# Retention values and gate projected by one 512-column job at the head of the kernel

## The chip, the core and the metric

One Trainium2 chip, one core of it. The metric is the time of one execution of the whole program on the device, in microseconds (us). Five engines run side by side, each with its own queue of instructions, worked off in order: TensorE (PE in the profile, with its weight loads as PEld), VectorE (DVE), ScalarE (ACT), GpSimd (POOL) and SyncE (SP, which issues the DMAs). They wait for each other through semaphores.

## The reference, cut to what matters

A decoder layer: one projection of the input, three mixers side by side, an output projection, layer norm, an MLP and a second layer norm. All in float32, 1024 tokens of width 1024.

```python
z = x @ w_in                                        # 1024 x 1024 @ 1024 x 2816
u, rq, rk, rv, rg, aq, ak, av = jnp.split(z, ...)   # 256 columns each up to rg, then 512 each
y_ssm = rms_norm(s5_mixer(u, ...), ssm_norm)        # a complex diagonal scan over the tokens
y_ret = retention_mixer(rq, rk, rv, rg, ret_norm)   # chunks of 128 tokens; silu(rg) * norm(o)
y_att = rms_norm(dilated_attention_mixer(aq, ak, av), attn_norm)
h = concatenate([y_ssm, y_ret, y_att]) @ w_out
x = layer_norm(ALPHA * x + h)
x = layer_norm(ALPHA * x + square(relu(x @ w1)) @ w2)
```

`rv` (columns 768 to 1023 of `w_in`) are the values of the retention, `rg` (columns 1024 to 1279) is its gate. They lie side by side.

## The kernel before

A float32 product is made of three passes of TensorE: both operands are split into a rounded part and a rest (`hi` and `lo`), and `mm3` (L403) adds hi x hi, hi x lo and lo x hi in PSUM. The split of a weight tile is a cast on ACT (`whi`) and a subtraction (`wlo`) that `sub_lo` (L427) gives to DVE or POOL, whichever it thinks is free first. For the input the two parts are `XA` and `XB`, split tile by tile in `split_x` (L475) from the loaded `xt`.

The input projection is a list of jobs (`JOBS`, L53). A "chunk" job (`tm_groups`, L489) gives token-major results of 256 columns: eight token tiles of 128, each summed over eight pieces `k` of the contraction, with 24 matmuls of 256 columns, two tiles to a PSUM bank. A "tile" job (`fm_groups`, L504) gives 128 features by 512 tokens, with matmuls of 512 columns. The order is: rv (job 0), rk and rq for two halves, rg (job 5), u twice, av, then aq, ak and av for the attention. Job 0 is special: x tile 0 and the two weight chunks are loaded alternately in small pieces (`load_x` L463, `load_w` L516, `split_w` L538), so that TensorE can begin early. Results are taken out of PSUM by `ev_rv` (an ACT copy, L586) and `ev_rg` (ACT tanh into `rgth`, then a DVE `scalar_tensor_tensor` into `sg`, L592).

Beside these jobs run: `ssm_params` (L700), a long chain of small DVE instructions on `par` tiles, then products `V` and `CA`, with a few transposes on PE in between (`ps_prm`, `ps_vt`, `ps_c`) and small matmuls (`ps_k`) at its end; `ssm`, which begins with 32 matmuls into `ps_X` from the u jobs, then a scan on DVE and POOL (`X`, `park`, `Sx`, `wz`), ACT copies into `Ss` and matmuls into `ps_y`; `retention` in four steps of two chunks (PE `ps_z`, `ps_sT`, `ps_kv`, `ps_ro`, `ps_rT`; DVE `rkz`, `at`, `R`, `st`, `mv`, `on`; POOL `rst` and `on` times `sg`); the attention; and from about 400 us on the output projection (`MB` operands first, then `wah`/`wal`), then the MLP.

Nothing of this order is written out by hand. The parts are coroutines with a rank each, and a planner (`Stream`, L244) that runs when the program is built keeps an estimated clock for each engine and always emits the next instruction that could start earliest, ranks breaking ties. Ranks near 0 are the retention (0) and the S5 mixer (1); the projection jobs (10) fill the gaps on PE. The order so found is fixed in each engine's queue: on the chip an instruction that is not ready holds up all that stands behind it.

Of the kernel before, what the change touches and what calls it, by code (L numbers as in the profile page):

```python
# [13 lines left out]
F32R = mybir.dt.float32r  # L14
# [30 lines left out]
PICK = 2  # L45
NORMP = 0
ACTB = 0
JOBB = 15
VALA = 28
VALV = 4  # L50
WAG = "xb4.0"

JOBS = [("chunk", 768)] + [("tile", c + 128 * p) for p in range(2) for c in (512, 256)]  # L53
JOBS += [("chunk", 1024), ("tile", 0), ("tile", 128), ("chunk", 2304)]
JOBS += [("tile", c + 128 * p) for p in range(2) for c in (1280, 1792)] + [("chunk", 2560)]
JOBS += [("tile", c + 128 * p) for p in (2, 3) for c in (1280, 1792)]
LN2_HI = 0.693359375
# [240 lines left out]
async def when(w, early=0.0):  # L298
    if isinstance(w, str):
        await ask(("flag", w))  # L300
    elif w:
        await ask(("data", w, early))
# [3 lines left out]
def trunk_kernel(ctx: ExitStack, tc: tile.TileContext, t_in, out):  # L306
# [43 lines left out]
    def free(*tiles):  # L350

        for t in tiles:
            if isinstance(t, (list, tuple)):
                free(*t)
            else:
                room = st_.room[tags.pop(t.tensor.name)]
                room[0] += 1
                room[1].append(clock.last[t.tensor.name])
# [4 lines left out]
    async def Us(n, shape, dt=F32, name="u", spare=2):  # L363
        return [await U(shape, dt, name, spare) for _ in range(n)]
# [62 lines left out]
    async def sub_lo(lo, raw, hi, pick=PICK):  # L427

        await when([hi, raw])
        n = int(np.prod(lo.shape[1:]))  # L430
        t, r = clock.t, clock.ready([hi, raw], [lo])
        r = max(r, t.get("port", 0.0))
        late = max(t.get("dve", 0.0), r) + pick + 0.00104 * n > max(t.get("pool", 0.0), r) + 0.0021 * n
        await tt(pool if late else dve, lo, raw, f(hi), SUB)
# [28 lines left out]
    async def load_x():  # L463
        for t in range(8):
            xts[t] = await U([128, NKT, 128], name="xt")
            for a in range(XP[t]):
                n = NKT // XP[t]
                k = slice(n * a, n * a + n)
                await sp.dma_start(out=xts[t][:, k], in_=x_t[t][:, k])
                flag(f"xload{t}.{a}")  # L470
                if t == 0:
                    await when(f"wload0.{a}")
            flag(f"xload{t}")

    async def split_x():  # L475
# [13 lines left out]
    async def tm_groups(hl, done):  # L489
        for tp in range(4):  # L490
            ps = await PM((128, 2, 256))
            for i in range(2):
                t = 2 * tp + i
                tok = slice(t * 128, (t + 1) * 128)
                for k in range(NKT):
                    if k % (NKT // XP[t]) == 0:
                        await when(f"x{t}.{k}")
                    if t == 0 and k % 2 == 0:
                        await when(f"w0.{k}")
                    wh, wl = hl[k // 4]  # L500
                    await mm3(ps[:, i], XA[:, k, tok], XB[:, k, tok], wh[:, k % 4], wl[:, k % 4], k == 0, k == NKT - 1)
            done(tp, ps)

    async def fm_groups(hl, done):  # L504
        wh, wl = hl[0]
# [5 lines left out]
            done(th, ps)  # L511

    wraw, wsplit = {}, {}
    w_shape = {"chunk": [128, 4, 256], "tile": [128, NKT, 128]}

    async def load_w():  # L516
        u = 0
        for j, (kind, _) in enumerate(JOBS):
            if j > 1:
                await when(f"job{j - LOADW}")  # L520
            wraw[j] = []
            for i in range(2 if kind == "chunk" else 1):
                src = w_in[u].rearrange("p (a b) -> p a b", a=w_shape[kind][1])
                u += 1
                raw = await U(w_shape[kind], name="wraw", spare=4 if j > 1 else 0)
                wraw[j].append(raw)
                if j == 0:
                    for k in range(0, 4, 2):
                        await when(f"xload0.{2 * i + k // 2}")
                        await sp.dma_start(out=raw[:, k:k + 2], in_=src[:, k:k + 2])  # L530
                        flag(f"wload0.{2 * i + k // 2}")
                else:
                    await sp.dma_start(out=raw, in_=src)
            flag(f"wload{j}")
            if j == 0:
                await when("xload5")

    async def split_w():  # L538
        for j, (kind, _) in enumerate(JOBS):
            if j == 0:  # L540
                whl = await Us(4, w_shape[kind], F32R, "w0", spare=0)
                wsplit[0] = [whl[0:2], whl[2:4]]
                flag("wsplit0")
                for i in range(2):
                    await when(f"wload0.{2 * i}")
                    raw, (hi, lo) = wraw[0][i], whl[2 * i:2 * i + 2]
                    for k in range(0, 4, 2):
                        await when(f"wload0.{2 * i + k // 2}")
                        await act.copy(hi[:, k:k + 2], raw[:, k:k + 2])
                        await sub_lo(lo[:, k:k + 2], raw[:, k:k + 2], hi[:, k:k + 2], 0.0)  # L550
                        flag(f"w0.{4 * i + k}")
                    free(raw)
                continue
            await when(f"wload{j}")
            await when(f"job{j - 1}")
            wsplit[j] = [await w_split(w, w_shape[kind]) for w in wraw.pop(j)]
            flag(f"wsplit{j}")

    async def evacuate(j, groups, evac, name, queue):
        for i in range(2 if groups is fm_groups else 4):  # L560
            await when(f"sum{j}.{i}")
            await evac(i, queue[i])
        if name:
# [19 lines left out]

    T = {}

    async def ev_rv(tp, ps):  # L586
        if tp == 0:
            T["rv"] = await Us(2, [128, 4, 256], name="rv", spare=0)
        await act.copy(T["rv"][tp // 2][:, 2 * (tp % 2):2 * (tp % 2) + 2], ps)
        free(ps)  # L590

    async def ev_rg(tp, ps):  # L592
        if tp == 0:
            T["sg"] = await Us(2, [128, 4, 256], name="sg", spare=0)
        th = await H([128, 2, 256], name="rgth")
        await act.activation(th, ps, AF.Tanh, scale=0.5)
        await stt(T["sg"][tp // 2][:, 2 * (tp % 2):2 * (tp % 2) + 2], th, 1.0, ps, A_, M)
        free(th, ps)

    def ev_rq(p):  # L600
# [50 lines left out]
        return g  # L651


    jobs = [(tm_groups, ev_rv, "rv")]
    for p in range(2):
        jobs += [(fm_groups, ev_rk(p), None), (fm_groups, ev_rq(p), None if p == 0 else "rqk")]
    jobs += [(tm_groups, ev_rg, "rg"), (fm_groups, ev_u(0), None), (fm_groups, ev_u(1), "u"), (tm_groups, ev_av(0), "av0")]

    def qk_jobs(p):
        return [(fm_groups, ev_qk(p, "aq", -0.125), None), (fm_groups, ev_qk(p, "ak", 1.0), f"qk{p}")]  # L660
# [419 lines left out]
    async def retention():  # L1080
# [7 lines left out]
        for np_ in range(4):  # L1088
# [72 lines left out]
                        mv[:, i, h, 0:1], rst[:, i, h:h + 1], SUB, M)  # L1161
            free(po, mv, rst)
            if sg is None:
                await when("rg")
                sg = T["sg"]
            await tt(pool, on, on, sg[np_ // 2][:, 2 * (np_ % 2):2 * (np_ % 2) + 2], M)
            await when([on])
# [967 lines left out]
def host_arrays(inputs):  # L2135

    src = {n: np.ascontiguousarray(inputs[n]) for n in _INS}
    kp = lambda w: w.reshape(w.shape[0] // 128, 128, -1).transpose(1, 0, 2)
    src["x_t"] = np.ascontiguousarray(inputs["x"][0].reshape(8, 128, 8, 128).transpose(0, 3, 2, 1))
    w = inputs["w_in"][0]  # L2140
    units = []
    for kind, c0 in JOBS:
        if kind == "tile":
            units.append(kp(w[:, c0:c0 + 128]))
        else:
            units += [kp(w[a * 512:(a + 1) * 512, c0:c0 + 256]) for a in range(2)]
    src["w_in_units"] = np.stack([np.ascontiguousarray(u).reshape(128, 1024) for u in units])
    src["mlp_w1_units"] = np.ascontiguousarray(
        inputs["mlp_w1"][0].reshape(8, 128, 32, 128).transpose(2, 1, 0, 3).reshape(32, 128, 1024))
    src["mlp_w2_units"] = np.ascontiguousarray(  # L2150
        inputs["mlp_w2"][0].reshape(8, 2, 2, 128, 2, 512).transpose(2, 4, 0, 3, 1, 5).reshape(4, 8, 128, 1024))
    two = lambda n: inputs[n][0].reshape((8, 2) + inputs[n].shape[2:])
    col = lambda n: inputs[n][0].reshape(-1, 128).T
    pad = lambda v: np.concatenate([v, np.zeros((128 - v.shape[0], v.shape[1]), v.dtype)])
    src["params"] = np.concatenate(
        [two("ssm_b_" + n).transpose(1, 2, 0, 3).reshape(128, 128) for n in ("re", "im")]
        + [two("ssm_c_" + n).transpose(0, 2, 1, 3).reshape(128, 128) for n in ("re", "im")]
        + [pad(inputs["ssm_d"][0].reshape(8, 2, 16).transpose(1, 2, 0).reshape(32, 8))]
        + [col(n) for n in ("ret_out_norm", "ssm_out_norm", "ssm_b_glu", "ssm_b_glu", "attn_out_norm")], 1)
    src["rates"] = np.concatenate([two("ssm_lambda_re").reshape(8, 128), two("ssm_lambda_im").reshape(8, 128),  # L2160
                                   two("ssm_log_dt")], 1)
    src.update(shape_tables())
    return src
# [16 lines left out]
```

## Time and profile before

| | us |
|---|---|
| median of 3 runs | 1170.29 (1166.64 to 1170.9) |
| the profiled execution, its own time | 1170.03 |
| its span in the trace | 1168.3 |
| PE busy | 1122.4 (96%) |
| DVE busy | 814.3 (70%) |
| ACT busy | 532.3 (46%) |
| POOL busy | 239.4 (20%) |

The span is what the engines' records cover; 1.7 us of the execution lie around it. The rows of a trace are of this one execution. A matmul's duration in them overlaps with the next one's: the pace of PE is the distance from start to start. "Idle before, releaser" is the time for which the engine had nothing to do before an instruction, and what it had waited for.

### The profile page before, as it was taken

What the parts mean: (1) busy time and instruction counts of PE and PEld (TensorE: products, weight loads), DVE (VectorE), ACT (ScalarE), POOL (GpSimd) and SP (SyncE); (2) the same over time, 40 slices, a digit from 0 to 9 for tenths busy, and PEclk for the clock granted to TensorE, in tenths of its full rate; (3) what the DMA queues carried; (4) which work ended last, traced back from release to release, by engine and by line L of the source; (5) the groups of instructions that cost most, each with busy time, mean ns of one, the idle gap of its engine ahead of it and who ended that gap; (6) DMA issues with size and microseconds to landing.
All of it is one profiled execution on the core that took longest, in us unless ns stands there. A gap on an engine that the chain in (4) does not pass through costs nothing.

```text
span 1168.3 us, 15903 instructions
## 1 busy us (share of the span) xinstructions
PE 1122.4 (96%) x5825; PEld 950.5 (81%) x5825; DVE 814.3 (70%) x1665; ACT 532.3 (46%) x941; POOL 239.4 (20%) x183
## 2 busy tenths in 40 slices
PE   8999999899999989999999999999999999999996
PEld 7889888778888777887778888888788888888875
DVE  5986567676563688899776766667457785675865
ACT  5121322676756657336445454545444343442530
POOL 1232316635164533466000000000000000000104
PEclk9999999899999999999999999999999999999989
DMA  8000421520151624034263444434598667767521
GB/s 320 19 1 31 137 74 49 194 92 19 37 182 64 226 90 153 33 122 163 98 219 143 173 150 155 156 142 154 180 350 333 199 202 248 270 223 263 191 81 72
DMA packets 65133, 175.36 MB, mean 150 GB/s; under 512 B 7064, under 2 KB 16800, under 8 KB 65056
## 3 DMA queue, kind: packets, MB, share of 16 engines
q1 hardware_dynamic: 65056, 174.35, 42.6%
q8 instruction: 46, 0.75, 0.3%
q14 instruction: 31, 0.25, 0.1%
HBM read 127.42 MB, written 46.91 MB: 149 GB/s over the span
## 4 chain that ended last, share of the span: by engine, by line
PE 44%; DVE 4%; DMA 1%; issue 1%; ACT 1%; SPq 0%; DVEq 0%; POOL 0%
PE ps L394 27%; PE pm L394 17%; DVE dol L234 1%; DVE X L234 1%; DMA wraw<-in_mlp_w_units 1%; DMA rraw<-r_d 0%; DVE rs L234 0%; DMA K<-in_mlp_w_units 0%; DVE wop L234 0%; DVE SQ L234 0%; DVE ws L234 0%; ACT rb L234 0%; ACT X L234 0%; ACT doh L234 0%; DVE rb L234 0%
## 5 line engine op out<-in xcount | busy, mean ns | idle before, releaser
L234 POOL TENSOR_TENSOR lnr<-lnr,nhalf 128x1 f32<-128x1 f32 x16 | 10.9, 684 | 592.8 <-DVE lnmv L234 530.1
L394 PE MATMUL ps<-xoh,wop 128*128 128x512 f32 x384 | 123.7, 390 | 1.8 <-DVE u L234 1.8
L394 PE MATMUL pm<-doh 128*128 128x512 f32 x256 | 100.9, 394 | 3.0 <-DVE X L234 3.0
L234 ACT CAST doh<-rraw 128x1024 fp32r<-128x1024 f32 x56 | 58.7, 1049 | 93.2 <-DMA rraw<-r_d 73.2
L394 PE MATMUL pm<-dol,doh 128*128 128x512 f32 x256 | 100.8, 394 | 0.0
L394 PE MATMUL pm<-doh,dol 128*128 128x512 f32 x256 | 100.7, 393 | 0.0
L394 PE MATMUL pm<-XOB,wop 128*128 128x512 f32 x384 | 95.2, 393 | 0.2 <-DVE wop L234 0.2
L394 PE MATMUL ps<-XOA,wop 128*128 128x512 f32 x384 | 91.2, 390 | 3.6 <-DVE wop L234 3.6
L234 DVE TENSOR_TENSOR dol<-rraw,doh 128x1024 fp32r<-128x1024 f32 x56 | 68.4, 1221 | 33.0 <-ACT doh L234 33.0
L394 PE MATMUL pm<-XA,whi 128*128 128x512 f32 x224 | 89.3, 399 | 0.0
L394 PE MATMUL pm<-XA,wlo 128*128 128x512 f32 x224 | 88.6, 396 | 0.0
L394 PE MATMUL pm<-XB,whi 128*128 128x512 f32 x224 | 88.5, 395 | 0.0
L394 PEld LDWEIGHTS ps<-XOA,wop 128*128 128x128 f32 x384 | 71.9, 188 | 19.7 <-DVE wop L234 4.8
L394 PEld LDWEIGHTS ps<-xoh,wop 128*128 128x128 f32 x384 | 72.1, 188 | 17.4 <-DVE u L234 2.2
L234 ACT ACTIVATE rb<-rb 128x512 f32<-128x512 f32 x64 | 40.5, 633 | 98.6 <-DVE rb L234 97.6
L394 PEld LDWEIGHTS pm<-XOB,wop 128*128 128x128 f32 x384 | 71.0, 188 | 14.6 <-DVE wop L234 0.6
L234 POOL TENSOR_TENSOR wlo<-wraw,whi 128x1024 fp32r<-128x1024 f32 x24 | 58.3, 2440 | 104.2 <-ACT whi L234 83.9
L394 PE MATMUL ps<-xol,wop 128*128 128x512 f32 x192 | 74.7, 389 | 0.0
L394 PE MATMUL ps<-doh 128*128 128x512 f32 x192 | 74.7, 389 | 0.0
L394 PE MATMUL ps<-dol,doh 128*128 128x512 f32 x192 | 74.7, 389 | 0.0
L394 PE MATMUL ps<-doh,dol 128*128 128x512 f32 x192 | 74.7, 389 | 0.0
L394 PEld LDWEIGHTS pm<-doh 128*128 128x128 f32 x256 | 48.6, 190 | 14.3 <-issue 2.8
(286 smaller groups left out, 2802.9 us busy)
## 6 DMA issues: line engine op xcount, KB each, us to landing
wraw<-in_mlp_w_units SPq DMA_DIRECT2D x92, 512.0 KB
rraw<-r_d SPq DMA_DIRECT2D x56, 512.0 KB
r_d<-rs SPq DMA_DIRECT2D x32, 512.0 KB
wraw<-in_w_in_units SPq DMA_DIRECT2D x20, 512.0 KB
v_d<-v SPq DMA_DIRECT2D x8, 512.0 KB
w<-v_d SPq DMA_DIRECT2D x8, 512.0 KB
abias<-in_c_bias SPq DMA_DIRECT2D x8, 512.0 KB
wraw<-in_w_out SPq DMA_DIRECT2D x8, 512.0 KB
```

Source lines behind the costliest of these rows:

```text
L234: fn(*a, **kw)
L394: nc.tensor.matmul(ps, a, b, start=start, stop=stop, skip_group_check=open_)
```

## The change

rv and rg become one job, the first: eight token tiles, each with 24 matmuls of 512 columns into a whole PSUM bank (`wide_groups`), 192 in place of 2 x 192 of 256 columns. Its weights are four units of 256 rows by 512 columns, loaded in eight pieces (one for each `k`) instead of four pieces of two; x tile 0 is loaded as before, between them. `ev_rvg` takes the left half of each bank with an ACT copy and the right half with tanh on ACT and the multiply on DVE: eight of each on 256 columns, in place of four of each on 512. The job of rg after rq is gone, and so u follows rq directly. `JOBB` counts the same job as before.

```diff
-JOBB = 15
+JOBB = 14
-JOBS = [("chunk", 768)] + [("tile", c + 128 * p) for p in range(2) for c in (512, 256)]
-JOBS += [("chunk", 1024), ("tile", 0), ("tile", 128), ("chunk", 2304)]
+JOBS = [("wide", 768)] + [("tile", c + 128 * p) for p in range(2) for c in (512, 256)]
+JOBS += [("tile", 0), ("tile", 128), ("chunk", 2304)]
...
+    async def wide_groups(hl, done):
+        for t in range(8):
+            ps = await PM()
+            tok = slice(t * 128, (t + 1) * 128)
+            for k in range(NKT):
+                if k % (NKT // XP[t]) == 0:
+                    await when(f"x{t}.{k}")
+                if t == 0:
+                    await when(f"w0.{k}")
+                wh, wl = hl[k // 2]
+                await mm3(ps, XA[:, k, tok], XB[:, k, tok], wh[:, k % 2], wl[:, k % 2], k == 0, k == NKT - 1)
+            done(t, ps)
...
-                    for k in range(0, 4, 2):
-                        await when(f"xload0.{2 * i + k // 2}")
-                        await sp.dma_start(out=raw[:, k:k + 2], in_=src[:, k:k + 2])
-                        flag(f"wload0.{2 * i + k // 2}")
+                    await when(f"xload0.{i}")
+                    for k in range(2):
+                        await sp.dma_start(out=raw[:, k], in_=src[:, k])
+                        flag(f"wload0.{2 * i + k}")
...
-    async def ev_rv(tp, ps):
-        if tp == 0:
+    async def ev_rvg(t, ps):
+        if t == 0:
             T["rv"] = await Us(2, [128, 4, 256], name="rv", spare=0)
-        await act.copy(T["rv"][tp // 2][:, 2 * (tp % 2):2 * (tp % 2) + 2], ps)
-        free(ps)
-
-    async def ev_rg(tp, ps):
-        if tp == 0:
             T["sg"] = await Us(2, [128, 4, 256], name="sg", spare=0)
-        th = await H([128, 2, 256], name="rgth")
-        await act.activation(th, ps, AF.Tanh, scale=0.5)
-        await stt(T["sg"][tp // 2][:, 2 * (tp % 2):2 * (tp % 2) + 2], th, 1.0, ps, A_, M)
+        th = await H([128, 256], name="rgth")
+        await act.copy(T["rv"][t // 4][:, t % 4], ps[:, 0:256])
+        await act.activation(th, ps[:, 256:512], AF.Tanh, scale=0.5)
+        await stt(T["sg"][t // 4][:, t % 4], th, 1.0, ps[:, 256:512], A_, M)
         free(th, ps)
...
-    jobs = [(tm_groups, ev_rv, "rv")]
+    jobs = [(wide_groups, ev_rvg, "rv")]
...
-    jobs += [(tm_groups, ev_rg, "rg"), (fm_groups, ev_u(0), None), (fm_groups, ev_u(1), "u"), (tm_groups, ev_av(0), "av0")]
+    jobs += [(fm_groups, ev_u(0), None), (fm_groups, ev_u(1), "u"), (tm_groups, ev_av(0), "av0")]
```

Because the planner orders everything, the change moves instructions far beyond these lines. From the last part of the attention on (3004 PE instructions before the end, of 5421 now and 5613 before) PE's order is the same in both; ahead of that it is not. Three places.

VectorE at the start, between the split of x (`XB`) and the first instructions of the S5 parameters (`par`). Before:

```order
L234 TENSOR_TENSOR XB<-xt,XA 128x4x128 x2
L234 TENSOR_TENSOR XB<-xt,XA 128x8x128 x6
L234 COPY cols<-small 128x12
L234 COPY par<-small 8x256
L234 TENSOR_SCALAR cols<-cols 128x2 x3
L234 COPY par<-small 8x128
L234 COPY par<-ps_prm 128x24
```

and now:

```order
L234 TENSOR_TENSOR XB<-xt,XA 128x4x128 x2
L234 SCALAR_TENSOR_TENSOR sg<-rgth,pm 128x256
L234 TENSOR_TENSOR XB<-xt,XA 128x8x128 x4
L234 SCALAR_TENSOR_TENSOR sg<-rgth,pm 128x256
L234 TENSOR_TENSOR XB<-xt,XA 128x8x128 x2
L234 SCALAR_TENSOR_TENSOR sg<-rgth,pm 128x256
L234 COPY cols<-small 128x12
L234 COPY par<-small 8x256
L234 TENSOR_SCALAR cols<-cols 128x2 x3
L234 COPY par<-small 8x128
L234 COPY par<-ps_prm 128x24
```

Three of the eight gate instructions, each of which waits for a token tile of job 0, now stand ahead of the S5 parameters; the other five stand inside that chain, before its last `V`, out of which three `rq` instructions have moved to behind it.

GpSimd from the start on: its first work, the subtractions `wlo` of the job weights, and what follows. Before:

```order
L234 MEMSET zr 32x448
L234 TENSOR_TENSOR wlo<-wraw,whi 128x1024 x7
L234 MEMSET R 128x1024 x2
L234 TENSOR_TENSOR rst<-rst,nhalf 128x8
L234 MEMSET par 128x256 x2
```

and now:

```order
L234 MEMSET zr 32x448
L234 TENSOR_TENSOR wlo<-wraw,whi 128x1024 x4
L234 MEMSET par 128x256
L234 TENSOR_TENSOR wlo<-wraw,whi 128x1024
L234 MEMSET par 128x256
L234 TENSOR_TENSOR par<-ident 32x16
L234 MEMSET R 128x1024 x2
```

Since job 0 is longer, fewer of these weight splits fall into the time of the S5 parameters: on ACT, whose cast `whi` each `wlo` waits for, the first stands behind the tanh of the second token tile, the second behind that of the seventh, the third behind the first `rk`, the fourth behind two of the four copies out of `ps_vt`.

VectorE at the beginning of the S5 scan (`X`, `park`). Before, the scan follows the last `on` of the fourth retention step and runs through:

```order
L234 TENSOR_SCALAR on<-ps_ro,mv,rst 128x64 x8
L234 TENSOR_TENSOR park<-X,park 128x128 x4
L234 TENSOR_TENSOR park<-park 128x128 x2
L234 TENSOR_TENSOR X<-X,park 128x128 x2
L234 TENSOR_TENSOR park<-X,park 128x128 x4
```

and now it follows the third:

```order
L234 TENSOR_SCALAR on<-ps_ro,mv,rst 128x64 x8
L234 TENSOR_TENSOR park<-X,park 128x128 x4
L234 TENSOR_TENSOR park<-park 128x128 x2
L234 TENSOR_TENSOR X<-X,park 128x128 x2
L234 TENSOR_TENSOR park<-X,park 128x128 x4
L234 TENSOR_TENSOR rkz<-ps_z,tabs 128x512
L234 TENSOR_TENSOR park<-park 128x128 x2
L234 TENSOR_TENSOR X<-X,park 128x128 x2
L234 TENSOR_TENSOR park<-X,park 128x128 x2
L234 TENSOR_TENSOR at<-ps_sT,tabs 128x512 x2
```

The whole fourth retention step is now spread over the scan. On PE, between the last matmul into `ps_X` and the first into `ps_y`, stood 165 matmuls of 256 columns, 93 of 512 and four transposes into `ps_rT`; now 149 of 256, 143 of 512 and one whole retention step more. On POOL the two pairs `wz` and `Sx` of the scan have one `wlo` and one `v` between them and, ahead of them, a `wlo` and two more `v`; before, they had one `wlo` and one `v` between them and nothing ahead.

## Rows read from the trace of the kernel before

**Rows 1.** The page, busy time and share of each engine.

```profile
PE 1122.4 (96%) x5825; PEld 950.5 (81%) x5825; DVE 814.3 (70%) x1665; ACT 532.3 (46%) x941; POOL 239.4 (20%) x183
```

**Rows 2.** A stretch: bounds, length; busy PE, PEld, DVE, ACT, POOL; clock; DMA.

```profile
30.00:520.00 490.00, 467.89 (x2860) 408.31 (x2860) 350.78 (x1029) 236.11 (x515) 197.00 (x145) 0.99 0.27 90
```

**Rows 3.** Waits of PE from 30 to 520 us: total, times, longest.

```profile
PE ps_k L394 <- DVE par L234: 0.9, 2, 0.6
...
PE ps_X L394 <- DMA UT<-u_d: 0.9, 1, 0.9
```

**Rows 4.** Timeline of PE, three stretches: start, us, instruction, count, idle before.

```profile
11.86 0.41 PE L394 MATMUL pm<-w,XB 128*128 128x256 f32 x1
...
12.50 0.41 PE L394 MATMUL pm<-w,XB 128*128 128x256 f32 x1
...
32.95 0.28 PE L394 MATMUL pm<-w,XB 128*128 128x256 f32 x1
33.07 0.40 PE L394 MATMUL pm<-XA,whi 128*128 128x512 f32 x1
...
36.50 0.39 PE L394 MATMUL pm<-XA,whi 128*128 128x512 f32 x1
37.18 0.39 PE L394 MATMUL pm<-XA,whi 128*128 128x512 f32 x1
```

**Rows 5.** Timeline of ACT: the last cast of job 0's weights.

```profile
9.21 0.62 ACT L234 CAST w<-wraw 128x512 fp32r<-128x512 f32 x1
```

**Rows 6.** Stretches of the start, columns as in rows 2, GB/s at the end.

```profile
0.00:10.00 10.00, 4.42 (x15) 3.51 (x16) 3.73 (x8) 5.25 (x10) 1.28 (x9) 1.00 0.77 228
10.00:15.00 5.00, 5.00 (x33) 5.00 (x33) 3.99 (x5) 3.26 (x4) 0.00 (x0) 1.00 1.02 418
```

**Rows 7.** Timeline of DVE in the S5 parameters, and of POOL.

```profile
26.73 0.18 DVE L234 COPY par<-ps_prm 128x24 f32<-128x24 f32 x1 [4.39 <-PE ps_prm L400]
...
50.37 0.68 DVE L234 TENSOR_TENSOR rq<-pm,tabs 128x512 f32<-128x512 f32 x1
...
51.17 2.48 DVE L234 TENSOR_TENSOR par<-park 128x16 f32<-128x16 f32 x2
...
73.90 0.28 DVE L234 TENSOR_TENSOR V<-V,vw 128x128 f32<-128x128 f32 x1
...
51.23 2.39 POOL L234 TENSOR_TENSOR wlo<-wraw,whi 128x1024 fp32r<-128x1024 f32 x1 [8.49 <-ACT whi L234]
```

**Rows 8.** Timeline of PE: three waits, and the matmuls behind them.

```profile
74.24 0.66 PE L400 MATMUL ps_vt<-ident,V 128*128 128x128 f32 x4 [0.86 <-DVE V L234]
...
208.83 0.80 PE L394 MATMUL ps_y<-Cs,Ss 128*128 128x128 f32 x2 [3.94 <-ACT Ss L234]
...
415.48 4.15 PE L394 MATMUL pm<-MB 128*128 128x512 f32 x10 [2.34 <-POOL MB L234]
```

**Rows 9.** Stretches: the two batches into `ps_y`, and the attention.

```profile
208.83:215.00 6.17, 6.17 (x31) 6.17 (x32) 1.11 (x2) 2.23 (x3) 1.26 (x1) 0.55 0.63 201
219.25:222.70 3.45, 3.45 (x32) 3.45 (x31) 2.68 (x4) 1.83 (x3) 3.38 (x2) 1.00 0.74 267
230.00:470.00 240.00, 225.73 (x1328) 196.16 (x1327) 162.04 (x452) 159.61 (x406) 98.83 (x87) 0.99 0.31 107
```

**Rows 10.** DVE groups of the retention, 84 to 165 us: busy, mean ns, idle before.

```profile
L234 DVE TENSOR_SCALAR on<-ps_ro,mv,rst 128x64 f32<-128x64 f32 x32 | 8.4, 340 | 6.6 <-POOL rst L234 6.6
L234 DVE BATCH_NORM_STATS2 st<-ps_ro 128x6 f32<-128x64 f32 x32 | 6.5, 205 | 6.1 <-PE ps_ro L394 6.1
L234 DVE BATCH_NORM_AGGREGATE mv<-st 128x2 f32<-128x6 f32 x32 | 5.8, 181 | 0.8
L234 DVE SCALAR_TENSOR_TENSOR R<-R,ps_kv 64x64 f32<-64x64 f32 x24 | 5.2, 218 | 1.7 <-PE ps_kv L394 1.2
L234 DVE TENSOR_TENSOR at<-ps_sT,tabs 128x512 f32<-128x512 f32 x8 | 5.1, 686 | 1.9 <-PE ps_sT L394 1.9
...
L234 DVE TENSOR_TENSOR rkz<-ps_z,tabs 128x512 f32<-128x512 f32 x4 | 2.8, 692 | 9.9 <-PE ps_z L400 9.9
```

More of the change, by code (lines that the diff above doesn't have):

```diff
@@ L471, in load_x @@
                 if t == 0:
-                    await when(f"wload0.{a}")
+                    await when(f"wload0.{2 * a + 1}")
             flag(f"xload{t}")
@@ L495, in tm_groups @@
                 for k in range(NKT):
[L496 to L499, printed above, removed]
                     wh, wl = hl[k // 4]
@@ L513, in trunk_kernel @@
     wraw, wsplit = {}, {}
-    w_shape = {"chunk": [128, 4, 256], "tile": [128, NKT, 128]}
+    w_shape = {"wide": [128, 2, 512], "chunk": [128, 4, 256], "tile": [128, NKT, 128]}
     async def load_w():
@@ L521, in load_w @@
             wraw[j] = []
-            for i in range(2 if kind == "chunk" else 1):
+            for i in range({"wide": 4, "chunk": 2, "tile": 1}[kind]):
                 src = w_in[u].rearrange("p (a b) -> p a b", a=w_shape[kind][1])
@@ L540, in split_w @@
             if j == 0:
-                whl = await Us(4, w_shape[kind], F32R, "w0", spare=0)
-                wsplit[0] = [whl[0:2], whl[2:4]]
+                whl = await Us(8, w_shape[kind], F32R, "w0", spare=0)
+                wsplit[0] = [whl[i:i + 2] for i in range(0, 8, 2)]
                 flag("wsplit0")
[L544 to L551, printed above, removed]
+                for i, (hi, lo) in enumerate(wsplit[0]):
+                    for k in range(2):
+                        await when(f"wload0.{2 * i + k}")
+                        raw = wraw[0][i]
+                        await act.copy(hi[:, k], raw[:, k])
+                        await sub_lo(lo[:, k], raw[:, k], hi[:, k], 0.0)
+                        flag(f"w0.{2 * i + k}")
                     free(raw)
@@ L559, in evacuate @@
     async def evacuate(j, groups, evac, name, queue):
-        for i in range(2 if groups is fm_groups else 4):
+        for i in range({wide_groups: 8, tm_groups: 4, fm_groups: 2}[groups]):
             await when(f"sum{j}.{i}")
@@ L1163, in retention @@
             if sg is None:
-                await when("rg")
                 sg = T["sg"]
@@ L2144, in host_arrays @@
             units.append(kp(w[:, c0:c0 + 128]))
+        elif kind == "wide":
+            units += [kp(w[a * 256:(a + 1) * 256, c0:c0 + 512]) for a in range(4)]
         else:
```

## The prediction

> **What bounds the kernel now.** I read the page's busy line first. TensorE (PE) is busy for 1122 us of a span of 1168, 96%; no other engine passes 70% [rows 1]. So the time is PE's work plus PE's waits, and an edit counts only where it shortens the one or the other. From the last part of the attention on PE's order is the same in both programs, and I give that part nothing. Ahead of it, from 30 to 520 us, PE waits for 490 - 467.9 = 22 us [rows 2]; the table of waits and the timeline say for what [rows 3, 8]. The longest single wait is 3.94 us in front of the first matmul into `ps_y`, for `Ss`, the end of the S5 scan. The reader should also see what follows it: 31 matmuls take 6.17 us at a granted clock of 0.55, where 32 of the same batch take 3.45 us at full clock later [rows 9]. So that wait costs another 2.7 us at the lower level, 1.2 GHz. After the 2.34 us in front of `MB` ten matmuls of 512 columns take 4.15 us, where ten at .227 would take 2.27 [rows 8]: the same thing. A long wait of PE is paid nearly twice.
>
> **Paces.** Durations of matmuls overlap, so I count from start to start. A product (three matmuls) of 256 columns takes .64 us in the first microseconds (11.86 to 12.50); later one matmul of 256 takes .12 (32.95 to 33.07), the product .36; a product of 512 takes .68 (36.50 to 37.18), a matmul .227 [rows 4]. The same columns therefore cost 2 x .36 = .72 in two products of 256 and .68 in one of 512. The .64 is what 1.2 GHz would give (256 / 1.2 = 213 ns a matmul), although the stretches at the start show a granted clock of 1.00 [rows 6]; I go by the starts.
>
> **1. The start: +3.7 us.** Before, the last cast of job 0's weights begins at 9.21 [rows 5], tile 0 ends at about 12.1 and job 0 at 33.07 [rows 4]. rg's 64 products of 256 come later, at .36: 23.0 us. So the work that the wide job holds is done, in sum, as if at 33.1 + 23.0 = 56.1. Now x tile 0 (.52 MB) and all of the weights (2.10 MB) must arrive before tile 0 can end: 2.62 MB instead of 1.57. The first 10 us moved 2.28 MB, the next five went at 418 GB/s [rows 6]; the last .34 MB thus take about 1 us and land at 11. Before, 1.57 MB were in at about 7.5 (at the mean 228 GB/s it would be 6.9, but the queues start up first) and the last cast began 1.7 later; with the same lag it begins at 12.5-12.7. Adding one product with its `lo` part behind it, tile 0 ends at 14.3. Seven tiles of eight products at .68 follow: 14.3 + 38.1 = 52.4. The gain is 56.1 - 52.4 = 3.7, of which the wider matmuls alone make 64 x (.72 - .68) = 2.6; the rest is PE filling the load time with work. If the transfers go faster, tile 0 ends at 12.8 (gain 5.2); if PE runs at half pace through tile 0, eight products of 1.28 end at 15.1 (2.9). I take 3.7, by the transfers.
>
> The Trainium skill (TensorE: Matmul & The Clock Gate, Back-to-back issue gap) gives a single matmul the gap N / 2.4 + 2.5 ns: 109 ns for 256 columns and 216 for 512. By that, 192 wide ones in place of 384 would save 192 x 2.5 ns = .5 us and not 2.6, and the sum below would end near 1164.1, an estimate from that page. The trace has .120 and .227, and the measurement decides.
>
> **2. The wait for `V`: -0.4.** The S5 parameters begin when DVE gets `ps_prm`, at 26.73 after 4.39 us of waiting for PE [rows 7]. PE's queue, counted in the order of the changed program as all counts of "now" are, holds 62 matmuls of .227 between the end of tile 0 and `ps_prm`: 14.3 + 14.1 = 28.4, and the chain begins at 28.8, 2.1 later. It ended with the last `V` at 73.9 + .28 = 74.2 [rows 7], and PE, in order, waited .86 for that [rows 8]. What lies in the chain changes in two ways. Three `rq` of .68 [rows 7] leave it and five `sg` come in, of half of that each: -.3. And there are fewer stalls: two small instructions took 2.48 us beside a `wlo` of 2.39 on GpSimd, where .18 is usual for one [rows 7], so that each `wlo` stalls DVE by 2.1; five of them fell in there, now two, since the others wait for casts that stand behind the gate's tanh on ACT. That is -6.4. `V` is then there at 74.2 + 2.1 - .3 - 6.4 = 69.6. PE comes to `ps_vt` after 238 matmuls of 512 behind tile 0, at 14.3 + 54.0 = 68.3, and waits 1.3 in place of .86. The eight `sg` find their tiles ready: tile 3 is done at 14.3 + 3 x 5.44 = 30.6, when the chain has just begun.
>
> **3. The waits for `par` in front of `ps_k`: +0.9.** They total .9 [rows 3]. In the old order DVE did a first retention step and the gate between the last `V` and this point; both are gone from there, while PE keeps 82 matmuls of 512, 18.6 us. The wait should go. The one for `UT` (.9 [rows 3]) I leave as it is, between 0 and 1.8.
>
> **4. The scan: +3.9.** Here the moved order counts most. Between the last `ps_X` and the first `ps_y` PE had 165 matmuls of 256, 93 of 512 and four transposes: 165 x .12 + 93 x .227 + 4 x .108 = 41.3 us. Now it has 149 of 256 and 143 of 512, 50.3 us, and the 56 small matmuls of a retention step (at most 128 columns, .108 each as in the second `ps_y` batch [rows 9]), 6.0: 56.3, so 15.0 us more cover. Against that DVE does a retention step in the middle of the scan. The six large groups of four steps hold 8.4 + 6.5 + 5.8 + 5.2 + 5.1 + 2.8 = 33.8 us, 8.5 a step [rows 10]. Its own waits in the old place were 6.6 + 6.1 + 9.9 = 22.6, 5.7 a step [rows 10]; two `wlo` or `v` beside it on GpSimd could add 2 x 2.4 [rows 7]. So the step takes 8.5 plus something from 0 to 10.5. I take 4.0: the waits for PE in `rkz` and `st` (16.0 of the 22.6) have scan work to stand in them, which leaves 1.65 of `on`, and one `wlo`, 2.4. The wait becomes 3.94 + 8.5 + 4.0 - 15.0 = 1.4, 2.5 less; and a shorter wait should lose less clock: I take half of the 2.7, 1.35.
>
> **5. The rest: 0.** The other waits up to 520 us (of `MB`, `ps_o`, `ps_pt`) have the same work behind and ahead of them; what PE no longer has as filler in the attention I weigh as a rival.
>
> **Sum.** 3.7 - .4 + .9 + 3.9 = 8.1, against the profiled execution's own 1170.0 (1168.3 and 1.7 around it), which is within .3 of the median: **1162.0**. With the ends of terms 1 to 4 (2.9 to 5.2; up to 1.8 worse; the extra of the scan 2 more or less) about 1159 to 1166.5.
>
> **Rivals.** *B, the start is given back at `V`.* If four `wlo` stall the chain instead of two, because ACT's casts come earlier than its queue suggests, `V` ends 4.2 later, PE waits 5.5 and then runs for a while at half pace (some 2.0, by the two cases above): 4.2 + 2.0 = 6.2 above the sum, at 1168. For it: PE reaches `ps_vt` five microseconds earlier while the chain begins two later. Against: the casts stand behind evacuations that can't be early.
>
> *C, the scan becomes the end, and the kernel is slower.* DVE's step costs its full 10.5 and not 4.0: PE's in-order queue has `ps_kv` and `ps_ro` of that step in front of `ps_y`, and each of them waits for DVE, which has scan work ahead. The wait is then 7.9, 4.0 more than before; with its clock loss near 4, and 50 matmuls of 512 (11.3 us) that were filler later already used up, so that one more wait like that of `MB` (2.3 + 1.9) appears in the attention: 1170.0 - 4.2 (terms 1 to 3) + 4.0 + 1.3 + 4.2 = 1175. It turns against the change from an extra of about 9 on. For it: three engines meet in that step. Against: DVE is busy for only 162 of 240 us in the attention behind [rows 9], so there is room. The Trainium skill (SBUF: State Buffer, Who interferes with whom) has DVE instructions with two inputs in SBUF fully blocked while GpSimd reads there; the stalled pair in rows 7 agrees, 2.48 beside 2.39, and most of the scan's instructions are of that kind.
>
> *D, the cover is more than enough.* The extra is 0 to 2.6: the wait and the whole clock loss go (6.6 in place of 3.9), and with PE ahead elsewhere the waits for `MB` shrink too: 1157.
>
> **How the numbers follow.** Forecast .45, B .24, C .20, D .11. The likeliest is 1162.0. Leaving out the tails of C and D gives 1157 to 1175 for 8 in 10. A measurement of this kernel can tell .5% from no change, 5.9 us: faster is below 1164.4, slower above 1176.1. Faster: D, and three quarters of the forecast's range, .45; slower: the upper part of C, .11; the rest, .44, is the forecast's upper end, B and most of C.
>
> **What would show it.** Step 1: the last matmul of job 0 near 52.4, tile 0's end near 14.3, the products then .68. Step 2: `ps_vt` behind a wait of 1 to 2 us near 69, two long pairs in the chain and not five. Step 3: no `ps_k` among PE's waits. Step 4: `ps_y` behind a wait under 2 us, its first batch near 5 us. Step 5: the same list of waits from there to 520, in sum 13 to 15. I am wrong if the wait in front of `ps_y` grows, if a new long wait stands in front of `ps_ro` or `ps_kv` during the scan, or if PE stands idle for several microseconds at `ps_vt`: each brings the low clock along.

## The result, and the profile after

The changed kernel takes 1181.65 us (median of 6; 1179.21 to 1184.01) where the kernel before takes 1170.3: a ratio of 1.0108 (95% interval 1.0093 to 1.0123). It is slower by 11 us; forecast were 1162.0, with 1157 to 1175 as the range. The profiled execution is the longest of the six, 1184.01 with a span of 1182.2, so the trace shows 13.9 us more than the one before.

The page's busy line of after [rows 1]:

```profile
PE 1128.2 (95%) x5633; PEld 945.3 (80%) x5633; DVE 827.5 (70%) x1673; ACT 533.0 (45%) x951; POOL 237.3 (20%) x181
```

and the line on its core, span and mean granted clock:

```profile
core 0: 1182.2 us, clock 0.979
```

PE has 192 instructions less and is busy 5.8 us longer. It is idle for 1182.2 - 1128.2 = 54.0 us in place of 45.9. The mean clock was .991 before. By the paces of the prediction the wide matmuls save 2.6 us of busy time, so the low clock must have lengthened the matmuls by some 5.8 + 2.6 = 8.4 us (an estimate); 8.1 us of idle time come on top. Four stretches show where; the columns are those of [rows 2]. Before:

```profile
15.00:150.00 135.00, 133.24 (x903) 118.75 (x901) 94.27 (x374) 37.85 (x51) 35.24 (x21) 1.00 0.23 79
150.00:235.00 85.00, 79.31 (x527) 70.90 (x523) 60.70 (x163) 31.78 (x46) 41.65 (x18) 0.96 0.33 106
235.00:500.00 265.00, 250.34 (x1467) 217.05 (x1466) 185.10 (x481) 166.64 (x417) 111.90 (x97) 0.99 0.28 99
500.00:1150.00 650.00, 640.65 (x2856) 527.84 (x2855) 455.59 (x619) 287.47 (x416) 40.23 (x30) 0.99 0.54 189
```

After:

```profile
15.00:150.00 135.00, 134.26 (x768) 112.79 (x768) 88.90 (x364) 36.56 (x56) 28.00 (x17) 1.00 0.27 84
150.00:235.00 85.00, 78.37 (x504) 69.51 (x500) 65.43 (x172) 33.14 (x47) 45.34 (x20) 0.98 0.29 97
235.00:500.00 265.00, 242.60 (x1383) 209.69 (x1382) 186.02 (x471) 165.46 (x416) 104.98 (x93) 0.94 0.28 96
500.00:1150.00 650.00, 640.75 (x2866) 528.35 (x2865) 462.96 (x628) 288.81 (x418) 45.88 (x33) 0.99 0.54 190
```

The start and the end are as forecast: up to 150 us PE waits 1 us less, behind 500 nothing differs. The loss lies in the attention, 235 to 500 us: PE waits 265 - 242.6 = 22.4 us instead of 14.7, and the mean clock is .94 instead of .99; in none of the other three stretches did it fall. So nearly all of the 8.1 us and most of the 8.4 us arise there. The waits of after between 150 and 300 us [rows 3], with total, times and longest:

```profile
PE ps_rT L400 <- POOL on L234: 6.0, 2, 5.2
PE pm L394 <- POOL wlo L234: 4.8, 2, 3.1
PE ps_f L394 <- DVE stat L234: 2.5, 1, 2.5
PE ps_pt L400 <- DVE s L234: 1.9, 1, 1.9
PE ps_s L394 <- DVE stat L234: 0.7, 1, 0.7
```

`ps_y` is gone from the list, `ps_rT` is new in this size (its longest wait was .9 before). Then come waits of the attention, and one of the projection itself. PE's timeline at these places (start, us, instruction, idle before) [rows 4, 8]; the first line is the first matmul behind job 0:

```profile
53.27 0.39 PE L394 MATMUL pm<-XA,whi 128*128 128x512 f32 x1
...
70.04 0.66 PE L400 MATMUL ps_vt<-ident,V 128*128 128x128 f32 x4 [0.74 <-DVE V L234]
...
180.56 1.12 PE L400 MATMUL ps_rT<-ident,on 128*128 128x128 f32 x4 [5.24 <-POOL on L234]
...
218.20 0.38 PE L394 MATMUL ps_y<-Cs,Ss 128*128 128x128 f32 x2
...
258.18 0.62 PE L394 MATMUL ps_f<-KH,by_r 128*128 128x256 f32 x2 [2.49 <-DVE stat L234]
...
268.50 0.58 PE L394 MATMUL pm<-wlo,XA 128*128 128x256 f32 x1 [3.08 <-POOL wlo L234]
```

Why the attention suffers is seen in the projection matmuls (`pm`) alone, the work that PE does there while DVE and ACT make the softmax. In two stretches, 235 to 265 and 265 to 300 us, the busy time and count of `pm` (then clock and DMA), before:

```profile
235.00:265.00 30.00, 15.85 (x66) 1.00 0.28 92
265.00:300.00 35.00, 19.10 (x132) 1.00 0.04 14
```

and after:

```profile
235.00:265.00 30.00, 2.47 (x9) 0.89 0.20 71
265.00:300.00 35.00, 26.98 (x191) 0.85 0.09 31
```

Before, half of PE's time from 235 to 265 us was projection; now it is 2.5 us of 30. That work was done earlier: up to 235 us PE was busy with `pm` for 187.6 us, before for 178.8. And the next job can't start: its weights are split at 262.6 (ACT) and 266.1 (GpSimd), the cast behind the softmax in ACT's queue. PE meets waits of .7, 2.5 and 3.1 us with hardly any projection between them, and the mean clock of these 30 us is .89.

Why was it done earlier? The order is fixed when the program is built: the planner, which gives PE whatever could start earliest, put more projection matmuls ahead of `ps_y`. On the chip the scan is late too. DVE is through with `park` at 186.5, but the scan's tail goes through GpSimd, whose queue read, before:

```profile
184.86 2.90 POOL L234 TENSOR_TENSOR wz<-park 128x960 f32<-128x960 f32 x1 [20.99 <-DVE park L234]
187.69 2.82 POOL L234 TENSOR_TENSOR wlo<-wraw,whi 128x1024 fp32r<-128x1024 f32 x1
190.47 2.25 POOL L234 TENSOR_TENSOR Sx<-Sx,wz 128x960 f32<-128x960 f32 x1
192.68 2.51 POOL L234 TENSOR_TENSOR wz<-park 128x960 f32<-128x960 f32 x1
195.14 3.05 POOL L234 TENSOR_TENSOR v<-av,v 128x512 fp32r<-128x512 f32 x1
198.15 3.17 POOL L234 TENSOR_TENSOR Sx<-Sx,wz 128x960 f32<-128x960 f32 x1
```

and after:

```profile
187.15 1.79 POOL L234 TENSOR_TENSOR v<-av,v 128x512 fp32r<-128x512 f32 x1 [6.65 <-ACT v L234]
188.90 2.40 POOL L234 TENSOR_TENSOR wlo<-wraw,whi 128x1024 fp32r<-128x1024 f32 x1
191.26 1.28 POOL L234 TENSOR_TENSOR v<-av,v 128x512 fp32r<-128x512 f32 x1
192.50 2.49 POOL L234 TENSOR_TENSOR wz<-park 128x960 f32<-128x960 f32 x1
194.94 1.29 POOL L234 TENSOR_TENSOR v<-av,v 128x512 fp32r<-128x512 f32 x1
196.19 2.26 POOL L234 TENSOR_TENSOR Sx<-Sx,wz 128x960 f32<-128x960 f32 x1
198.41 2.53 POOL L234 TENSOR_TENSOR wz<-park 128x960 f32<-128x960 f32 x1
200.91 2.39 POOL L234 TENSOR_TENSOR wlo<-wraw,whi 128x1024 fp32r<-128x1024 f32 x1
203.25 2.25 POOL L234 TENSOR_TENSOR Sx<-Sx,wz 128x960 f32<-128x960 f32 x1
```

and DVE and ACT around it:

```profile
155.04 2.33 DVE L234 TENSOR_TENSOR park<-X,park 128x128 f32<-128x128 f32 x4
...
185.96 0.59 ACT L234 COPY av<-pm 128x512 f32<-128x512 f32 x1 [3.41 <-PE pm L394]
186.44 1.15 ACT L234 CAST v<-av 128x512 fp32r<-128x512 f32 x2
...
186.44 1.35 DVE L234 COPY Sx<-X 128x896 f32<-128x896 f32 x2
...
198.49 8.87 DVE L234 TENSOR_TENSOR wz<-park 128x960 f32<-128x960 f32 x1 [10.44 <-POOL Sx L234]
...
216.00 2.12 ACT L234 COPY Ss<-Sx 64x1024 f32<-64x1024 f32 x2 [0.22 <-DVE Sx L234]
```

Five instructions of the projection and the values (`v`, `wlo`) stand ahead of and between the four of the scan, 9.2 us of them before the second `Sx`; before there were two, 5.9 us. A `wz` of DVE takes 8.87 us beside such work (the next takes 4.21). From its first product to the last `Ss` the scan takes 155.0 to 218.1, 63 us; before it took 47 (162.4 to 209.8). Of the difference 9.0 us fall before `park` is through (31.5 us, before 22.5), where the fourth retention step stands in between, and 6.6 us behind it.

The wait at `ps_rT` has a part in this. While PE stands there until 180.56, the job of av behind it stands too; its results reach ACT at 185.96, the cast of `v` follows, and GpSimd, idle for 6.65 us, can begin its first `v` at 187.15 only. `wz`, whose `park` is ready at 186.5, stands behind that `v`, a `wlo` and another `v`, and begins at 192.5.

PE spent the time on projection matmuls and so came to `ps_y` without a wait. The Trainium skill (SBUF — State Buffer, Who interferes with whom) says that a DVE instruction with two inputs in SBUF contends with a GpSimd instruction that reads SBUF. The lengths of `wz` on DVE agree: 8.87 us while GpSimd works without a gap over .2 us, and 1.88 us in the run e5 below, at 194.1, while GpSimd is idle.

### The profile page after: what moved, and what is told of

Read it like the earlier page. It is cut to its first block, busy times and chain, and to the rows that moved or that the text cites. A ratio compares the mean times of both kernels' runs of the same rounds, so it can differ in the third digit from the quotient of the medians.

```text
span 1182.2 us, 15529 instructions
## 1 busy us (share of the span) xinstructions
PE 1128.2 (95%) x5633; PEld 945.3 (80%) x5633; DVE 827.5 (70%) x1673; ACT 533.0 (45%) x951; POOL 237.3 (20%) x181
## 4 chain that ended last, share of the span: by engine, by line
PE 44%; DVE 4%; DMA 1%; issue 1%; ACT 1%; SPq 0%; POOL 0%; DVEq 0%; ACTq 0%
PE ps L394 27%; PE pm L394 17%; DVE dol L234 1%; DVE X L234 1%; DMA wraw<-in_mlp_w_units 1%; DMA K<-in_mlp_w_units 0%; DMA rraw<-r_d 0%; DVE rs L234 0%; DVE wop L234 0%; DVE SQ L234 0%; DVE ws L234 0%; ACT rb L234 0%; ACT X L234 0%; DVE rb L234 0%; DVE u L234 0%
## 5 line engine op out<-in xcount | busy, mean ns | idle before, releaser
L394 PEld LDWEIGHTS ps<-xoh,wop 128*128 128x128 f32 x384 | 72.1, 188 | 16.6 <-DVE u L234 1.6
L394 PEld LDWEIGHTS pm<-XOB,wop 128*128 128x128 f32 x384 | 71.0, 188 | 14.7 <-DVE wop L234 0.7
L234 POOL TENSOR_TENSOR wlo<-wraw,whi 128x1024 fp32r<-128x1024 f32 x22 | 54.4, 2491 | 103.6 <-ACT whi L234 64.3
```

Source lines behind the costliest of these rows:

```text
L234: fn(*a, **kw)
L394: nc.tensor.matmul(ps, a, b, start=start, stop=stop, skip_group_check=open_)
```

## The experiments

All ratios are to runs of the kernel before on the same chip (medians of 1168.6 to 1169.6 us there, 1170.3 beside after); times of different runs are compared by their ratios where it matters. "PE idle" is a stretch's length less PE's busy time, in the profiled execution; `pm` is its busy time from 235 to 265 us.

| kernel | median | ratio (95%) | PE idle 150-235 | PE idle 235-500 | clock 235-500 | `pm` |
|---|---|---|---|---|---|---|
| before | 1170.3 | | 5.7 | 14.7 | .99 | 15.9 |
| after | 1181.65 | 1.0108 (1.0093-1.0123) | 6.6 | 22.4 | .94 | 2.5 |
| e1_tie0 | 1178.69 | 1.0090 (1.0068-1.0112) | 6.4 | 19.6 | .96 | 9.6 |
| e2_rg_early | 1177.80 | 1.0075 (1.0051-1.0098) | 7.3 | 20.2 | .98 | 8.9 |
| e3_halves | 1181.98 | 1.0112 (1.0093-1.0131) | 6.6 | 22.2 | .95 | 3.2 |
| e4_before_tie0 | 1169.11 | 1.0006 (.9992-1.0019) | 6.0 | 12.4 | .99 | 17.1 |
| e5_scan_first | 1160.85 | .9934 (.9911-.9957) | 8.7 | 9.1 | .99 | 16.6 |
| e6_ret_first | 1184.48 | 1.0133 (1.0111-1.0154) | 16.2 | 19.3 | .97 | 10.1 |
| e7_dummy48 | 1177.51 | 1.0068 (1.0045-1.0090) | 6.6 | 13.6 | .98 | 13.7 |
| e8_before_scan_first | 1178.77 | 1.0083 (1.0062-1.0103) | 10.3 | 14.9 | .99 | 12.7 |
| e9_early_scan | 1177.12 | 1.0072 (1.0049-1.0096) | 10.4 | 13.1 | .99 | 18.8 |
| e10_scan_dummy48 | 1177.62 | 1.0073 (1.0055-1.0090) | 8.7 | 13.2 | .99 | 15.3 |
| e11_scan_fine | 1170.87 | 1.0014 (1.0003-1.0025) | 6.4 | 18.7 | .98 | 19.5 |
| e12_late_rt | 1168.11 | .9995 (.9985-1.0005) | 13.6 | 9.7 | 1.00 | 14.4 |

**Is it the change, or one unlucky order?** The planner's tolerance, which has nothing to do with the change, gives another order of the same work:

```diff
-TIE = 0.02
+TIE = 0.0
```

> The changed kernel with one number of the planner altered: of two instructions that could start at nearly the same time it now takes the earlier one always (tolerance 0 in place of 0.02 us). Same work, same jobs, another order, mostly in the attention. Theory M (rg ahead of rk and rq makes retention and scan late; the projection matmuls used up as cover lack in the attention, whatever the fine order): 1178 to 1185, ps_y at 216 to 220 us and the waits of 240 to 300 us near 10 us as now. Theory O (the loss is the particular order that the planner found in the attention): 1167 to 1173, ps_y as late, but the two stretches of 13.7 us at 1.2 GHz gone.

> The kernel before with the same tolerance 0: what another order of the same work does there. M: within 3 us of 1170. O: orders by chance differ by 10 us, so anything from 1165 to 1182.

The changed kernel gains 3 us by it, which the two intervals don't separate from nothing, the other nothing: at that point the loss seemed to belong to the change. **rg early, without the wide job** (the job of rg in second place, 256 columns):

```diff
-    jobs = [(tm_groups, ev_rv, "rv")]
+    jobs = [(tm_groups, ev_rv, "rv"), (tm_groups, ev_rg, "rg")]
...
-    jobs += [(tm_groups, ev_rg, "rg"), (fm_groups, ev_u(0), None), ...
+    jobs += [(fm_groups, ev_u(0), None), ...
```

> The kernel before, with the job of rg moved to second place, directly behind rv, both still with matmuls of 256 columns. M: slower than before by 10 us or more (1180 to 1186), since rk and rq come 23 us later and nothing is gained at the start. O: 1165 to 1176, as an order by chance. Rival W (the wide job itself, its longer load or its eight evacuations, is what costs): 1170.

It loses 9 us with no wide job in it, between the ranges of M and O, and PE's wait at `ps_rT` is there too (4.2 us). Up to 235 us PE was busy with `pm` for 187.0 us, as in after. So this order shows the pattern of the loss without the eight evacuations and the longer load. By its time alone it would prove little: orders of the kernel before reach the same ratio by chance, as the tolerances below show. **The wide matmul by itself:**

```diff
-    await mm3(ps, XA[:, k, tok], XB[:, k, tok], wh[:, k % 2], wl[:, k % 2], k == 0, k == NKT - 1)
+    for a, b, n in ((XA, wh, 0), (XA, wl, 1), (XB, wh, 2)):
...
+        for c in (slice(0, 256), slice(256, 512)):
+            nc.tensor.matmul(ps[:, c], a[:, k, tok], b[:, k % 2, c], start=k == 0 and n == 0, ...)
...
```

> The changed kernel with each matmul of 512 columns in job 0 as two of 256 behind each other, the rest of the order kept. By the paces of the trace (.24 for two, .2267 for one) 192 of them cost 2.6 us more if nothing hides it: job 0 ends 2.2 to 2.6 us later and the whole takes 1182 to 1185. By a fixed 2.5 ns a matmul it would be .5 us.

(The sums of its left halves lack their first product; no matmul is left out.) PE's timeline in it:

```profile
16.58 0.64 PE L513 MATMUL pm<-w,XA 128*128 128x256 f32 x4
...
17.30 0.64 PE L513 MATMUL pm<-w,XA 128*128 128x256 f32 x4
```

A product in halves takes .72 us where the wide one takes .68 (14.68 to 15.36 in after): the forecast's paces hold. But job 0 ends 1.2 us later (54.47 to 53.27) and not 2.2 to 2.6, since PE came to its faster pace at about 10.6 us here and at 12.5 in after. The whole differs by .3 us; the intervals, some 2 us to either side, can't tell that from 1.2.

**The fourth retention step and the scan.** In the next two the fourth step waits for the scan's end, or the scan for the fourth step:

```diff
+        flag("scan")                        # e5
         Sx = await restack(Sx, "Ss")
...
             await when([rk[1], rq[1]])
+            if np_ == 3:
+                await when("scan")
```

```diff
         await when([X[1], X[0]])
+        await when("ret")                   # e6
```

> The changed kernel with one rule more: the fourth retention step begins only when the S5 scan is through. Theory S (what costs is the fourth step inside the scan: it makes the scan late, PE waits 5.2 us for it at ps_rT, and the projection matmuls used as cover lack later): the first ps_y near 207 to 210 in place of 218, no wait at ps_rT, the stretches at 1.2 GHz between 250 and 300 us gone, 1165 to 1172. Theory L (rg ahead makes all of the retention 23 us late, and where the fourth step stands doesn't matter): 1177 to 1183.

> The opposite: the changed kernel, with the S5 scan begun only when all four retention steps are through, as the kernel before has it. S: the wait at ps_rT stays or shifts, the scan ends later still, ps_y near 222 to 228, and the time is 1180 to 1190. If it were the interleaving of the two on DVE alone (each holding up the other), not the lateness of the scan, it would be near 1172.

The first takes 21 us off the changed kernel, more than expected, and beats the kernel before by .66%; 1160.85 is what the forecast wanted. Its GpSimd has one `v` among the scan's four instructions in place of five others:

```profile
180.00 2.91 POOL L234 TENSOR_TENSOR wz<-park 128x960 f32<-128x960 f32 x1 [4.84 <-DVE park L234]
182.86 1.67 POOL L234 TENSOR_TENSOR v<-av,v 128x512 fp32r<-128x512 f32 x1
184.50 2.26 POOL L234 TENSOR_TENSOR Sx<-Sx,wz 128x960 f32<-128x960 f32 x1
186.71 2.48 POOL L234 TENSOR_TENSOR wz<-park 128x960 f32<-128x960 f32 x1
189.27 3.90 POOL L234 TENSOR_TENSOR Sx<-Sx,wz 128x960 f32<-128x960 f32 x1
```

The scan ends 19 us earlier, and PE waits for it, 4.4 us, then 2.9 for a `wlo`; up to 235 us it is busy with `pm` for 178.1 us, 9.5 less than in after:

```profile
198.31 0.77 PE L394 MATMUL ps_y<-Cs,Ss 128*128 128x128 f32 x2 [4.38 <-ACT Ss L234]
```

Its stretch of the attention, columns as in [rows 2]:

```profile
235.00:500.00 265.00, 255.93 (x1507) 224.37 (x1507) 192.79 (x500) 167.98 (x420) 118.65 (x103) 0.99 0.30 107
```

So it waits more than after does ahead of 235 us (8.7 to 6.6), and 13 us less behind it. In the second, `ps_y` waits 13.7 us at 225.9 and the attention is hardly better (19.3), although only 180.1 us of projection were spent by 235: the waits there have other sources too.

**Does PE lack work in the attention?** 48 matmuls whose results nothing uses, behind the projection of aq for the second pair of heads, in the changed kernel (e7) and in e5 (e10):

```diff
             await groups(hl, done)
+            if j == 10:
+                for _ in range(1):
+                    await fm_groups(hl, lambda i, ps: free(ps))
             free(hl)
```

> The changed kernel with 48 matmuls of 512 columns more, of no use, behind the projection job of aq for the second pair of heads: 48 x .227 = 10.9 us of work for PE, ready without any wait. If PE lacks cover in the attention (S and L alike), most of them stand where it waits or runs at 1.2 GHz: 1176 to 1185, at most 3 us more than now. If PE's waits there had another cause or cost nothing, the 10.9 us come on top: 1192.

10.9 us of work more, and 4.1 us less time. The waits of 235 to 500 fall by 8.8 us and the clock rises to .98, since PE has something to do at the place that had lost its `pm`:

```profile
235.00:265.00 30.00, 13.65 (x44) 1.00 0.27 92
265.00:300.00 35.00, 24.36 (x161) 1.00 0.08 28
```

> The changed kernel with the fourth step behind the scan, and with the same 48 useless matmuls (10.9 us) at the same place as in the run with them. If that kernel no longer lacks cover, they come on top but for the few waits left: 1168 to 1172. If useless matmuls had helped the changed kernel for another reason (a kinder order, a warmer PE in general), it would stay below 1164.

Where the attention is not short of work the same 48 matmuls cost 16.8 us, their own 10.9 and 4 us of waits. That is 6 us more than expected. Each of the two is one order, but they differ by 21 us: useless work helped only against the lack.

**Only the last instruction group of the step held back:**

```diff
+        flag("scan")                        # as in e5
...
             await when([on])
+            if np_ == 3:
+                await when("scan")
             ps = await PS((128, 2, 256), "ps_rT")
```

> The changed kernel with only the end of the fourth retention step (the transposes ps_rT and what follows) held back until the scan is through; its DVE work stays inside the scan. This takes away PE's wait of 5.2 us at ps_rT and leaves the scan late. If the wait and the clock behind it are the loss (5.2 + .9): 1174 to 1177. If the late scan is: 1179 to 1183. If all of it is this one instruction in PE's queue: 1165 to 1170.

13.5 us less, more than the 5.2 us of the wait and its clock. PE now waits 8.1 us for `Ss`, then 4.1 for a `wlo` (at 218.2):

```profile
150.00:235.00 85.00, 71.39 (x463) 64.17 (x463) 70.06 (x169) 31.95 (x46) 45.66 (x20) 0.94 0.27 91
235.00:500.00 265.00, 255.35 (x1495) 220.45 (x1494) 182.71 (x493) 167.06 (x419) 114.15 (x99) 1.00 0.30 104
```

Its idle time from 150 to 235 is twice that of after, and the time is 13.5 us better, since 12.7 us of waits and nearly all of the low clock behind 235 are gone. The first `ps_y` came at 208.3. PE did not stand at `ps_rT`, so the results of av reached ACT at 178.0 in place of 186.0 and GpSimd was through with `v` when `park` came. The planner had also moved the `v` and `wlo` from between `wz` and `Sx`, so this is not the wait alone.

**The other program, and the fine order.** The rule of e5 in the kernel before, in the narrow kernel with rg early, and in the changed kernel with two numbers of the planner altered:

```diff
 # e8: before; e9: as e2; e11: the changed kernel. In all three:
+        flag("scan")
...
+            if np_ in (3,):
+                await when("scan")
 # e11 alone:
-TIE = 0.02
+TIE = 0.01
-JOBB = 14
+JOBB = 15
```

> The kernel before with the rule of the first of these runs: the fourth retention step behind the scan. There the fourth step stood ahead of the scan and the scan began no later for it, since u came last. S: nothing to be won, 1167 to 1178. If scan first were simply a better order for any start: 1160 to 1165.

> rg directly behind rv with matmuls of 256 columns (as in the run with rg early), and the fourth retention step behind the scan. The difference to the wide job with the same rule (1160.9) is what the wide job itself gives at the start. If S holds for any early rg, and the start gains the 3.7 us of the prediction: 1164 to 1167. If the wide job gains nothing: 1161. If scan first only suited the order that the planner found there: 1172 or more.

> The changed kernel with the fourth step behind the scan, the planner's tolerance .01 in place of .02 and the projection's count for the output job (JOBB) 15 in place of 14: the same work, another fine order behind 250 us. By the spread that such numbers made before (3 us): 1155 to 1164.

The rule that won 21 us is no better order in itself: in the kernel before it costs 10 us; in the narrow kernel with rg early it wins nothing, since the waits of the attention fall (20.2 to 13.1) but those ahead of it and the low clock there grow (7.3 to 10.4, .98 to .92); and with two small numbers of the planner changed its gain shrinks by 10 us, against the expectation, although the scan ends at the same time (the last pair of `Ss` begins at 197.2 in both e5 and e11). The additional waits lie in the attention (18.7 in place of 9.1). That made the question of chance open again. So the tolerance alone, in both programs:

```diff
-TIE = 0.02
+TIE = 0.01    # and 0.03, 0.05
```

> The changed kernel with the planner's tolerance .01: another fine order. If the loss belongs to the change: 1176 to 1184, with the wait of 5 us at ps_rT. If it is chance: anything from 1160 to 1184.

> The same with .03. If the loss belongs to the change: 1176 to 1184. If chance: 1160 to 1184, and the five tolerances spread by 10 us or more.

> The same with .05. If the loss belongs to the change: 1176 to 1186. If chance: 1160 to 1184.

> The kernel before with the planner's tolerance .01. If the loss belongs to the change: 1165 to 1173. If orders by chance differ by 10 us in any program: as likely 1175 as 1169.

> The kernel before with .03. If the loss belongs to the change: 1165 to 1173, as with .02 and 0. If orders by chance differ by 10 us in any program: as likely 1175 as 1169.

> The kernel before with .05. If the loss belongs to the change: 1165 to 1173. If chance: as likely 1175 as 1169.

| tolerance | 0 | .01 | .02 | .03 | .05 | mean |
|---|---|---|---|---|---|---|
| before, ratio | 1.0006 | 1.0047 | 1 | 1.0088 | 1.0070 | 1.0042 |
| after, ratio | 1.0090 | 1.0089 | 1.0108 | 1.0114 | 1.0171 | 1.0114 |
| after, PE's longest wait at `ps_rT` | 5.1 | 5.1 | 5.2 | 3.2 | 5.4 | |
| before, `pm` busy up to 235 us | 179.0 | 179.1 | 178.8 | 178.9 | 178.4 | 178.8 |
| after, `pm` busy up to 235 us | 184.9 | 185.2 | 187.6 | 187.2 | 187.0 | 186.4 |
| before, PE idle 235-500 | 12.4 | 14.7 | 14.7 | 19.1 | 15.4 | 15.3 |
| after, PE idle 235-500 | 19.6 | 18.5 | 22.4 | 21.5 | 27.6 | 21.9 |

Orders of one program by chance span .8 to .9% in either: the new ones of the kernel before take 1173.7 to 1178.2, outside the 1165 to 1173 of the other theory. Still the changed kernel is slower at each tolerance, by .72% in the mean (8.4 us); with five orders of each, the 95% interval of that is about .2 to 1.25%. The pattern is in all five as well: a wait of over 3 us at `ps_rT` (before has .9 at most), none at `ps_y` (before has 3.9 to 4.2 us in each), 6 to 9 us more of projection spent by 235 us, and a mean of 6.7 us more waits behind it, at a clock of .94 to .97 in place of .98 to .99. The rest of the 1.08% is that the order at .02 is, with that at 0, the best of the five for the kernel before.

## Why the prediction was wrong

**Steps 1 to 3 held.** Job 0 ended at 53.27 (forecast 52.4), `ps_vt` came at 70.04 behind .74 us (69.6 and 1.3), two long pairs in DVE's chain and not five, no `ps_k` among the waits. The start thus gained 56.1 - 53.3 = 2.8 us of the 3.7, just under its lower end of 2.9: tile 0 ended at 14.68 (14.3), and the 56 products behind it took 38.6 (38.1). The .04 us that the wide matmul saves on a product is what [rows 4] gave. The Trainium skill (TensorE: Matmul & The Clock Gate, Back-to-back issue gap) gives a matmul by itself a fixed 2.5 ns beyond its columns; the trace has 13 for each matmul saved, and the measurement decides.

**Step 4 was half right.** The wait at `ps_y` fell, to nothing rather than 1.4. But the step's price to the scan was mis-sized: not 8.5 + 4.0 but 63.1 - 47.5 = 15.6 us, 8.5 and 7.1, where 7.1 lies within the ends 0 to 10.5 that the text gave and nearer the upper. The value was picked with one `wlo` in mind; three `v` and two `wlo` came, in an order that was known, and 6.6 of the 15.6 us arose in that part. And the wait moved rather than went: PE's in-order queue had `ps_rT` of the same step in it, where it stood for 5.24 us, which the forecast saw as a way to be wrong (it named `ps_ro` and `ps_kv`) and did not price. That wait also held up GpSimd by way of av and `v`.

**Step 5, "The rest: 0", failed.** The extra 15 us of cover that step 4 counted as a gain were projection matmuls taken from the attention, and the sum took them without paying them back. 235 to 500 us cost 7.7 us more of waits and most of the estimated 8.4 us by which the low clock lengthened the matmuls. The waits from the first `ps_y` to 520 us were to stay at 13 to 15 us in sum; they came to 22.4 (before 14.7). Rival C had this mechanism, with a chance of .20, but tied to a long wait at `ps_y`, which never came, and priced at one wait (4.2 us); its 1175 is 7 us short.

**Rival B** did not happen, nor D.

**The reader's error to avoid** is in the choice of 1162 as likeliest. It is the time of this change in a good order: e5 takes 1160.85. That the two numbers agree is luck: with two small numbers of the planner changed, the same rule takes 1170.87. The order that a planner finds moved the same work over 1160.9 to 1188.8 us, so a forecast that costs the edit exactly and the re-ordering by three places was too sure of itself; the range should have gone up by the 5 to 10 us that an order is worth here.

**What stays open.** How the mean loss of 8.4 us divides between GpSimd's queue in the scan, the wait at `ps_rT` and the emptied stretch, which hang together: each rule that takes one away makes the planner move the others. Why e6 and e11 wait for 19 us in the attention, with only 180 us of projection spent by 235, is not shown. The lack of `pm` from 235 to 265 is not the only form: at the tolerance .03 the changed kernel has 18.4 us of `pm` there, waits 21.5 us in the attention all the same, and takes 1182.13.

## What to carry to other kernels

Filler work that hides one wait is gone for the next: before counting "more cover here" as a gain, look at which later stretch gives it up, and whether the clock falls there too. Where a planner orders everything, price an edit in several orders of the same work (a changed tolerance is enough) before trusting one. And look at what stands in the queue of a helper engine between two links of a chain: here five small instructions on GpSimd, 9.2 us, stood between the scan's products and its results, where there had been two.

## What the runs showed of the hardware

By the mean granted clock, the same work ran with (1 - .979) x 1182 x 2 = 50 us at 1.2 GHz in after and (1 - .990) x 1159 x 2 = 23 us in e5 (estimates, with 1.2 and 2.4 GHz as the only levels). From 265 to 300 us after had 6.7 us of waits and a mean clock of .85, e12 2.7 us and 1.00: there, waits of a few us in all were paid again in clock. And at the start the granted clock is given as 1.00 while products of 512 columns come every 1.28 us (11.25 to 12.53), and every .7 from there on.
